# The fp32 products of 32 single rows: two weight tiles in one burst of 16 instead of one tile in a burst of 8

## The chip, the cores and the metric

One Trainium2 chip, one of its cores. The kernel is one launch. The time is device microseconds of one execution; the median of three executions of the kernel before is 1000.25 us (1000.03 to 1001.18). The profiled execution is another one, with its own time.

## What is computed

One inference step of a hybrid decoder layer for two groups of rows with the same weights: a prompt of 512 rows and a sample group of 8 x 4 = 32 rows. Cut to the matrix products that matter here:

```python
z = rms_norm(x, g_mix_pre) @ w_in            # q, k, v, o and gates of the mLSTM; dq, dk, dv of the attention
mix = concat(mlstm(z), diff_attention(z))    # with state and paged cache for the sample rows
x = x + rms_norm(mix @ w_out, g_mix_post)
x = x + rms_norm(mem_attend(rms_norm(x, g_mem_pre), mk, mv, w_mq, w_mo), g_mem_post)
u = rms_norm(x, g_ffn_pre) @ w_up            # (1024, 2*2752)
y = (silu(g) * a) @ w_down                   # after a causal depthwise convolution; (2752, 1024)
x = x + rms_norm(y, g_ffn_post)
```

Everything is fp32 in the reference. The outputs are the rows of both groups, the new caches and the states.

## The kernel before

**Two precisions.** For the 512 prompt rows a product is made of three fp32r matmuls. Each operand is split into a high part (a cast on ScalarE, line 142) and a low part (source minus high part, on VectorE or GpSimd, line 143); the three matmuls are high x high, high x low and low x high (lines 386 to 388 in `gemmA`, 1638 to 1640 in the down products). The 32 single rows, the sample group, do without the split: their products are plain fp32, from the weight tile as it came from memory.

**Weight tiles.** A weight tile is 256 x 512 (or 1024 x 128 for `gemmB`), 512 KB. The SP queue loads it into one of six stage buffers (`wst`, lines 227 and 246), ScalarE and VectorE split it into one of four slots (`wslot`). The class `Weights` holds a plan of all tiles in order: `W.get()` gives the next one, `W.free()` lets the plan run one tile further. A tile that `slotA` makes is the pair (slot, stage buffer), since the sample rows read the stage buffer. So a stage buffer is free once the split has read it and the sample products, if any, too.

**`gemmA`** makes a row-major projection of 512 columns: four weight tiles of two k each, for each tile the row blocks 0 to 3 of the prompt (128 rows each, 24 matmuls of 128 x 512 for a tile) and block 4, the sample rows. It is called for v (line 717), for dk, dq and dv (line 776), for the out projection and for mo (lines 1130 and 1136). Where a call is block-major (out, and the second half of mo) it follows another branch. `late=True` is used for the first half of mo.

**`sample_mm`** (line 366) makes the sample products of one weight tile: four fp32 products, two k times two column halves, of 128 x 256 each. Each goes to its own 32 partitions of one PSUM bank, so it uses 32 columns of TensorE's array. `sample_sum` (line 371) adds the four groups at the end.

**The ConvFFN** makes the up projection with `gemmB` (line 452; 440 for its first tiles) and after each group of four column tiles of the hidden width the down products of that group: two column halves (`n0`) of two weight tiles each, into five PSUM banks, one for each row block. There are six groups: four of them have four tiles and go through the loop `if not last`, so does the short one (tiles 20 and 21, third in order); the last one goes through `chunk`, block by block.

**What sets the order.** The program's order is a proposal only: the tile framework simulates a timeline and gives each engine its list of instructions, so work of several stages is interleaved on TensorE. In the stretch that makes dk, dq and dv it mixes their matmuls with the transposes of the rotated rows (line 742) and with the mLSTM head's chunks: mld (788, 789), mls (796), mlk (823), mlu (839), mli (857), mln (864), with mlD's activations on ScalarE (793) between.

The edit lengthens the file: three lines more in `gemmA`, nine by the end of the down products. A row of the changed kernel that reads L1647 is L1638 of before, L455 is 452, L745 is 742, L796 is 793, L842 is 839, L863 is 860.

## Time and profile before

| | us |
|---|---|
| median of three executions | 1000.25 |
| lowest, highest | 1000.03, 1001.18 |
| profiled execution, its time | 1001.39 |
| profiled execution, span from its first to its last instruction | 999.6 |
| mean granted TensorE clock | 0.988 of full speed |
| memory read and written | 112.22 MB, 16.93 MB |

The profile is one execution with every instruction's start. PE is TensorE's matmul pipe, PEld its weight loads, DVE VectorE, ACT ScalarE, POOL GpSimd, SP the queue that issues DMAs. A row of a timeline reads: start in us, us, engine, line and operation, output <- inputs, stationary operand, moving operand, count; in brackets the idle time before it and what ended it. The ends of matmuls are modelled, their starts are measured. A group of rows (by line and operation) gives count, busy time, the mean of one in ns and idle time ahead.

### The profile page before, as it was taken

What the parts mean: (1) busy time and instruction counts of PE and PEld (TensorE: products, weight loads), DVE (VectorE), ACT (ScalarE), POOL (GpSimd) and SP (SyncE); (2) the same over time, 40 slices, a digit from 0 to 9 for tenths busy, and PEclk for the clock granted to TensorE, in tenths of its full rate; (3) what the DMA queues carried; (4) which work ended last, traced back from release to release, by engine and by line L of the source; (5) the groups of instructions that cost most, each with busy time, mean ns of one, the idle gap of its engine ahead of it and who ended that gap; (6) DMA issues with size and microseconds to landing.
All of it is one profiled execution on the core that took longest, in us unless ns stands there. A gap on an engine that the chain in (4) does not pass through costs nothing.

```text
span 999.6 us, 17060 instructions
## 1 busy us (share of the span) xinstructions
PE 970.7 (97%) x6615; PEld 811.2 (81%) x6615; DVE 599.6 (60%) x1129; ACT 389.3 (39%) x746; POOL 196.1 (20%) x389
## 2 busy tenths in 40 slices
PE   8999999999799999999999999999999999999994
PEld 5899777889555778998767789989987997997983
DVE  5835324643586457643653578827848685775677
ACT  5654313434376447633552444242212222222232
POOL 6610000112332114500000264301101110010115
PEclk9999999999799999999999999999999999999997
DMA  8950234151634167785851673143143214215013
GB/s 278 296 162 14 72 85 130 43 183 55 176 109 136 61 210 233 250 260 166 277 214 43 195 237 107 43 129 91 41 115 87 84 46 127 90 42 145 25 47 110
DMA packets 120401, 130.26 MB, mean 130 GB/s; under 512 B 8423, under 2 KB 85832, under 8 KB 120320
## 3 DMA queue, kind: packets, MB, share of 16 engines
q1 hardware_dynamic: 114136, 125.69, 41.0%
q10 hardware_dynamic: 6184, 3.48, 1.2%
q8 instruction: 52, 0.85, 0.4%
q14 instruction: 29, 0.24, 0.1%
HBM read 112.22 MB, written 16.93 MB: 129 GB/s over the span
## 4 chain that ended last, share of the span: by engine, by line
PE 84%; DMA 5%; DVE 5%; issue 2%; POOL 1%; ACT 1%; SPq 0%; DVEq 0%; POOLq 0%; ACTq 0%
PE mm L452 31%; PE mm L386 6%; PE mm L387 6%; PE mm L388 6%; PE mm L440 5%; PE mm L1638 4%; PE mm L1640 4%; PE mm L1639 4%; PE mm L366 3%; PE sda L1179 2%; PE tpk L1384 2%; PE cpo L1365 1%; PE sca L1335 1%; PE ssc L1394 1%; PE oda L1205 1%
## 5 line engine op out<-in xcount | busy, mean ns | idle before, releaser
L142 ACT CAST wslot<-wst 128x1024 fp32r<-128x1024 f32 (+1 forms) x127 | 131.1, 1036 | 280.2 <-issue 81.5
L452 PE MATMUL mm<-fT,wslot 128*128 128x256 f32 (+1 forms) x1872 | 235.7, 288 | 0.0
L452 PEld LDWEIGHTS mm<-fT,wslot 128*128 128x128 f32 x1872 | 234.7, 188 | 0.7 <-issue 0.4
L143 DVE TENSOR_TENSOR wslot<-wst,wslot 128x1024 fp32r<-128x1024 f32 (+1 forms) x127 | 155.0, 1223 | 107.0 <-ACT wslot L142 106.9
L1638 PE MATMUL mm<-wslot,act 128*128 128x512 f32 (+1 forms) x176 | 70.7, 409 | 0.0
L1639 PE MATMUL mm<-wslot,act 128*128 128x512 f32 (+1 forms) x176 | 69.5, 395 | 0.0
L1640 PE MATMUL mm<-wslot,act 128*128 128x512 f32 (+1 forms) x176 | 69.0, 397 | 0.0
L1545 POOL COPY cvo<-u 128x2 f32<-128x2 f32 x43 | 16.2, 377 | 222.9 <-DVE u L1543 222.9
L386 PE MATMUL mm<-wslot,hT 128*128 128x512 f32 x128 | 51.9, 408 | 0.0
L452 PE MATMUL mm<-hT,wslot 128*128 128x288 f32 (+1 forms) x384 | 51.4, 290 | 0.0
L387 PE MATMUL mm<-wslot,hT 128*128 128x512 f32 x128 | 51.2, 400 | 0.0
L388 PE MATMUL mm<-wslot,hT 128*128 128x512 f32 x128 | 50.7, 397 | 0.0
L452 PEld LDWEIGHTS mm<-hT,wslot 128*128 128x128 f32 x384 | 48.9, 188 | 0.9 <-issue 0.8
L1638 PEld LDWEIGHTS mm<-wslot,act 128*128 128x128 f32 (+1 forms) x176 | 33.1, 189 | 17.7 <-issue 8.6
L1540 DVE TENSOR_TENSOR u<-mm,rsb 128x256 f32<-128x256 f32 x43 | 18.1, 423 | 43.5 <-PE mm L452 43.4
L1640 PEld LDWEIGHTS mm<-wslot,act 128*128 128x128 f32 (+1 forms) x176 | 33.0, 188 | 7.5
L1639 PEld LDWEIGHTS mm<-wslot,act 128*128 128x128 f32 (+1 forms) x176 | 33.1, 188 | 6.5
L1557 ACT ACTIVATE c<-c 128x560 f32<-128x560 f32 x21 | 14.1, 672 | 56.8 <-DVE c L1551 56.7
L1551 DVE SCALAR_TENSOR_TENSOR c<-u,cvT,c 128x560 f32<-128x560 f32 x43 | 34.3, 798 | 0.8
L1550 DVE SCALAR_TENSOR_TENSOR c<-u,cvT,c 128x560 f32<-128x560 f32 x43 | 34.1, 793 | 0.1
L1651 DVE TENSOR_TENSOR yp<-mm,yp 128x512 f32<-128x512 f32 x40 | 27.3, 688 | 9.5 <-PE mm L1640 9.4
L386 PEld LDWEIGHTS mm<-wslot,hT 128*128 128x128 f32 x128 | 24.0, 188 | 10.3 <-issue 5.8
(458 smaller groups left out, 1879.5 us busy)
## 6 DMA issues: line engine op xcount, KB each, us to landing
wst<-in_w_up_dram SPq DMA_DIRECT2D x42, 512.0 KB
wst<-in_w_in_dram SPq DMA_DIRECT2D x28, 512.0 KB
wst<-in_w_down_dram SPq DMA_DIRECT2D x20, 512.0 KB
wst<-in_cache_mem_k_dram SPq DMA_DIRECT2D x16, 512.0 KB
vt<-in_cache_mem_v_dram SPq DMA_DIRECT2D x8, 1024.0 KB
wst<-in_w_mk_dram SPq DMA_DIRECT2D x8, 512.0 KB
xb<-in_x_prompt_dram SPq DMA_DIRECT2D x8, 512.0 KB
wst<-in_cache_dk_dram SPq DMA_DIRECT2D x16, 256.0 KB
```

The costliest lines, as they stand in the source:

```text
L142: nc.scalar.copy(out=hi, in_=src)
L143: (eng or nc.vector).tensor_tensor(out=lo, in0=src, in1=f32(hi), op=SUB)
L386: mm(ps[b], lhsT=xt.hi(k, c0, c0 + n), rhs=s[:, 0, kk, :], start=(k == 0), stop=False)
L387: mm(ps[b], lhsT=xt.hi(k, c0, c0 + n), rhs=s[:, 1, kk, :], start=False, stop=False)
L388: mm(ps[b], lhsT=xt.lo(k, c0, c0 + n), rhs=s[:, 0, kk, :], start=False, stop=(k == nk - 1))
L440: mm(ps, lhsT=s[:, l, k, :], rhs=x(k, c0, c1), start=(k == 0 and j == 0), stop=(k == 7 and j == 2))
L452: mm(ps[i], lhsT=s[:, l, k, :], rhs=x(k, c0, c1), start=(k == 0 and j == 0), stop=(k == 7 and j == 2))
L1550: STT(out=c, in0=u[:, 1:EXT - 1], scalar=w[1], in1=c, op0=MUL, op1=ADD)
L1551: STT(out=c, in0=u[:, 0:EXT - 2], scalar=w[0], in1=c, op0=MUL, op1=ADD)
L1638: mm(ps, lhsT=t[:, 0, c0:c0 + P], rhs=s[:n, 0, i % 2, :], start=st, stop=False)
L1639: mm(ps, lhsT=t[:, 0, c0:c0 + P], rhs=s[:n, 1, i % 2, :], start=False, stop=False)
L1640: mm(ps, lhsT=t[:, 1, c0:c0 + P], rhs=s[:n, 0, i % 2, :], start=False, stop=en)
```

## The change

In `gemmA` outside the block-major branch the sample products of a weight tile are not issued when the tile comes, but kept in `behind`, and issued for two tiles when the second has come (k = 2 and k = 6). In the late form they are issued at k = 5 for all but the last tile kept, and at the end for the others. In the down products `one` keeps block 4's tiles in the same way and issues them at the second tile; the loops call it for block 4 only where i is even, once a weight tile. The number of products, their operands, and the bank and partitions that they go to are unchanged.

```diff
@@ gemmA
                     if 4 in blocks:
                         behind.append((k, s))
-                        if not late:
-                            one(4, *behind.pop(0))
+                        if k % 4 == 2 and not late:
+                            while behind:
+                                one(4, *behind.pop(0))
                 for b in blocks:
                     if b < 4:
                         one(b, k, s)
                 if k % 2 == 1:
-                    if len(behind) > 1:
-                        one(4, *behind.pop(0))
+                    if k == 5:
+                        while len(behind) > 1:
+                            one(4, *behind.pop(0))
                     if not late or k > 1:
                         W.free()
                 yield sum(0.64 if b < 4 else 0.43 for b in blocks)
             for k, s in behind:
                 one(4, k, s)
+            if behind:
                 W.free()
@@ down products
+        behind = []
+
         def one(b, ps, i, s):
...
             if b == 4:
-                if i % 2 == 0:
-                    sample_mm(ps, [acs[i], acs[i + 1]], s[1], st, i == nk - 2)
+
+                behind.append((i, s))
+                if i % 4 == 2 or i == nk - 2:
+                    for j, t in behind:
+                        sample_mm(ps, [acs[j], acs[j + 1]], t[1], j == 0, j == nk - 2)
+                    behind.clear()
                 return
...
                     for b in sorted(allb, reverse=i % 2 == 0):
-                        one(b, ps[b], i, s)
+                        if b < 4 or i % 2 == 0:
+                            one(b, ps[b], i, s)
...
-            for i in range(nk):
+            for i in range(0, nk, 2 if b == 4 else 1):
                 one(b, ps, i, wd[(n0 and nk // 2) + i // 2])
```

How the instructions stand on the engines, at three places. A name such as wst_6809 is one buffer of a tile, x4 a run of four equal rows; one row of L366 is one fp32 product.

TensorE at the start of the first down group, before: mm_7062 is the sample bank of the first column half, wst_6809 its first weight tile.

```order
L452 MATMUL mm_6984<-fT01_6087,wslot_6735 128x288
L366 MATMUL mm_7062<-wst_6809,acs_6607 32x256 x2
L366 MATMUL mm_7062<-wst_6809,acs_6615 32x256 x2
L1638 MATMUL mm_7061<-wslot_6810,act_6279 128x512
L1639 MATMUL mm_7061<-wslot_6810,act_6279 128x512
L1640 MATMUL mm_7061<-wslot_6810,act_6279 128x512
```

And after the change, where wst_6876 is the second weight tile of the same half:

```order
L1649 MATMUL mm_7058<-wslot_6810,act_6279 128x512
L366 MATMUL mm_7062<-wst_6809,acs_6607 32x256 x2
L366 MATMUL mm_7062<-wst_6809,acs_6615 32x256 x2
L366 MATMUL mm_7062<-wst_6876,acs_6757 32x256 x2
L366 MATMUL mm_7062<-wst_6876,acs_6899 32x256 x2
L1649 MATMUL mm_7060<-wslot_6877,act_6280 128x512
L1647 MATMUL mm_7059<-wslot_6877,act_6280 128x512
L1648 MATMUL mm_7059<-wslot_6877,act_6280 128x512
```

The first tile's products have moved from the group's first place to the second tile's, behind 29 fp32r matmuls.

TensorE at the end of dq, where the first sample products of dv (bank mm_1877) stand. Before:

```order
L386 MATMUL mm_1600<-wslot_1492,hT01_255 128x512
L387 MATMUL mm_1600<-wslot_1492,hT01_255 128x512
L388 MATMUL mm_1600<-wslot_1492,hT11_256 128x512
L366 MATMUL mm_1877<-wst_1630,xts_195 32x256 x4
L366 MATMUL mm_1877<-wst_1673,xts_195 32x256 x4
L864 MATMUL mln_1765<-vN_576,mlD_1428 128x129 x2
L742 MATMUL tpz_1808<-cpk_87,zq_1800 128x128 x4
```

After; wst_1626 and wst_1673 are dv's first two tiles:

```order
L386 MATMUL mm_1874<-wslot_1674,hT00_244 128x512
L387 MATMUL mm_1874<-wslot_1674,hT00_244 128x512
L366 MATMUL mm_1877<-wst_1626,xts_195 32x256 x4
L366 MATMUL mm_1877<-wst_1673,xts_195 32x256
L745 MATMUL tpz_1867<-cpk_87,zq_1856 128x32 x4
L842 MATMUL mlu_1892<-vN_576,wk_1699 128x129 x2
L366 MATMUL mm_1877<-wst_1673,xts_195 32x256 x3
L388 MATMUL mm_1874<-wslot_1674,hT10_245 128x512
```

The eight products stood together ahead of dv's fp32r matmuls; they now stand among them, and transposes and an mlu stand inside the run.

ScalarE in the dq stage, before: the casts (L142) are of dv's first three weight tiles, L793 is mlD of an mLSTM chunk.

```order
L744 COPY dkT<-tpz 128x4x128
L142 CAST wslot<-wst 128x1024
L744 COPY dkT<-tpz 128x4x32
L142 CAST wslot<-wst 128x1024
L793 ACTIVATE mlD<-mld,gt_1119 128x128 x4
L142 CAST wslot<-wst 128x1024
L464 COPY zq<-mm 128x512
```

And after:

```order
L747 COPY dkT<-tpz 128x4x128
L142 CAST wslot<-wst 128x1024
L747 COPY dkT<-tpz 128x4x32
L142 CAST wslot<-wst 128x1024 x2
L796 ACTIVATE mlD<-mld,gt_1119 128x128 x4
L863 ACTIVATE num<-mli,gt_1119 128x129 x2
L467 COPY zq<-mm 128x512
```

The third cast stands ahead of mlD's activations, where it stood behind them. On the SP queue the loads of dv's third and fourth tile stand behind all five stores of dk's rows, where the stores and loads alternated. GpSimd's order is the same.

## The prediction

> **What bounds the kernel now.** I read the page's busy times first, then its chain of waits. The first row is busy time and share of the span by engine; the other two are the chain that ended last, by engine and by line.

> ```profile
> PE 970.7 (97%) x6615; PEld 811.2 (81%) x6615; DVE 599.6 (60%) x1129; ACT 389.3 (39%) x746; POOL 196.1 (20%) x389
> ```
> ```profile
> PE 84%; DMA 5%; DVE 5%; issue 2%; POOL 1%; ACT 1%; SPq 0%; DVEq 0%; POOLq 0%; ACTq 0%
> PE mm L452 31%; PE mm L386 6%; PE mm L387 6%; PE mm L388 6%; PE mm L440 5%; PE mm L1638 4%; PE mm L1640 4%; PE mm L1639 4%; PE mm L366 3%; PE sda L1179 2%; PE tpk L1384 2%; PE cpo L1365 1%; PE sca L1335 1%; PE ssc L1394 1%; PE oda L1205 1%
> ```

> TensorE is busy for 97% of the span and 84% of the chain is its own work. But a share over the span says nothing of the stages that the change touches, so I asked for the busy time in windows. Columns: the window in us, its length, PE, PEld, DVE, ACT and POOL busy with their counts, the granted clock, the DMA share, GB/s.

> ```profile
> 97.00:225.00 128.00, 128.00 (x733) 98.23 (x726) 55.43 (x136) 40.38 (x76) 11.46 (x17) 1.00 0.36 102
> 253.00:285.00 32.00, 25.48 (x172) 16.00 (x172) 21.57 (x68) 15.42 (x48) 12.88 (x17) 0.79 0.55 165
> 259.00:273.00 14.00, 10.38 (x64) 6.46 (x65) 7.68 (x28) 1.88 (x6) 4.00 (x6) 0.51 0.68 204
> 640.00:960.00 320.00, 320.00 (x2212) 287.10 (x2211) 211.44 (x359) 81.71 (x99) 31.30 (x154) 1.00 0.29 81
> ```

> The projections v, dk, dq and dv lie in 97 to 225, the four down groups that change in 640 to 960. In both TensorE is never idle. So a nanosecond that its stream loses there is a nanosecond of the end, as long as nothing else becomes late. How many products there are does not change; the question is what a *burst* of them costs, and this the timeline shows.

> **What a burst costs.** Columns: start us, us, engine, line, operation. The profile records each fp32 product as two matmuls, so "x8" is four products, the four column groups of one weight tile. I call such a set of up to four a set.

> ```profile
> 649.06 0.39 PE L1639 MATMUL mm<-wslot,act 128*128 128x512 f32 x1
> 649.29 0.40 PE L1640 MATMUL mm<-wslot,act 128*128 128x512 f32 x1
> 649.62 0.64 PE L366 MATMUL mm<-wst,acs 128*32 128x256 f32 x8
> 650.18 0.50 PE L1638 MATMUL mm<-wslot,act 128*128 128x512 f32 x1
> 650.52 0.40 PE L1639 MATMUL mm<-wslot,act 128*128 128x512 f32 x1
> ...
> 658.40 0.40 PE L1640 MATMUL mm<-wslot,act 128*128 128x512 f32 x1
> 658.74 1.07 PE L366 MATMUL mm<-wst,acs 128*32 128x256 f32 x16
> 659.74 0.50 PE L1638 MATMUL mm<-wslot,act 128*128 128x512 f32 x1
> 660.07 0.39 PE L1639 MATMUL mm<-wslot,act 128*128 128x512 f32 x1
> ```
> ```profile
> 550.59 0.40 PE L388 MATMUL mm<-wslot,oT 128*128 128x512 f32 x1
> 550.91 2.80 PE L366 MATMUL mm<-wst,xts 128*32 128x256 f32 x48
> 553.64 0.50 PE L386 MATMUL mm<-wslot,oT 128*128 128x512 f32 x1
> 553.98 0.39 PE L387 MATMUL mm<-wslot,oT 128*128 128x512 f32 x1
> ```

> Ends are modelled, so I count from start to start. Two fp32r matmuls follow each other by 0.23 us (649.06 to 649.29). Around the burst of one set, 649.29 to 650.52 is 1.23; two steps of 0.23 belong to the fp32r matmuls, and 0.77 is the price of the burst. The burst of two sets: 658.40 to 660.07 is 1.67, less 0.46 is 1.21. That of six sets ("x48"): 550.59 to 553.98 is 3.39, less 0.46 is 2.93. From one set to six, (2.93 - 0.77) / 5 = 0.43 us for each further set, and two sets (1.21) lie on that line. What is left, 0.77 - 0.43 = 0.34 us, is paid once a burst: the last fp32r matmul before it, the first set and the two matmuls behind it start 0.33 apart where 0.23 is usual. So the kernel before already holds the merged form, and a merge saves 0.34 us.

> Two more readings decide how broken sets count. Columns as above.

> ```profile
> 162.56 0.62 PE L366 MATMUL mm<-wst,xts 128*32 128x256 f32 x2
> 163.11 0.50 PE L386 MATMUL mm<-wslot,hT 128*128 128x512 f32 x1
> ```
> ```profile
> 182.48 0.61 PE L857 MATMUL mli<-Cst,qT 128*128 128x129 f32 x4
> 182.93 0.61 PE L864 MATMUL mln<-vN,mlD 128*128 128x129 f32 x4
> ```
> ```profile
> 209.75 0.61 PE L857 MATMUL mli<-Cst,qT 128*128 128x129 f32 x4
> 210.28 0.62 PE L366 MATMUL mm<-wst,xts 128*32 128x256 f32 x4
> 210.84 0.60 PE L864 MATMUL mln<-vN,mlD 128*128 128x129 f32 x3
> ```

> One product alone holds the stream for 0.55 us (162.56 to 163.11), four for 0.56 (649.62 to 650.18): a set costs the same full or not, so breaking a set in two costs 0.43 more. And between fp32 matmuls of the mLSTM head the fixed part is smaller: 209.75 to 210.84 is 1.09, less 0.45 for the L857 group itself (182.48 to 182.93) is 0.64, less 0.43 for the set leaves 0.21.

> **The change part by part**, by the bursts in the order of the two kernels, each a number of products:

> - v: 4,4,4,4 becomes 8,8. Two bursts fewer, the same four sets: -0.68.
> - dk: the same, -0.68.
> - dq: 6,2,3,1,4 becomes 4,4,7,1. The scheduler drops other work between them, so the joint bursts do not stay whole. One burst fewer; six sets (2+1+1+1+1) become five: -0.34 - 0.43 = -0.77.
> - dv: 8,4,2,2 becomes 5,3,1,2,5. Here the order is worse than before: one burst and two sets more (5 to 7): +0.34 + 0.86 = +1.20.
> - the first half of mo: 2,2,4,24 becomes 8,24. Two bursts and one set fewer: -0.68 - 0.43 = -1.11.
> - the down products: each of the four large groups goes from 4,4,8 to 8,8, one burst fewer each: -1.36. The 8 before is the second column half, whose two tiles the scheduler already runs in one burst, so only half of what the diff seems to promise is there to be had. The group of two tiles and the last group keep their bursts, as does the out projection.

> Together ten bursts fewer (41 to 31) and no set fewer (-1 + 2 - 1): -3.4 us. If every one of the ten were worth only the 0.21 of the mLSTM rows, it would be -2.1. These are the two ends; I take 0.34, because dq and dv come to no burst in sum, and those of v, dk, mo and the downs lie between 512-wide fp32r matmuls like the row it is from.

> What else moves. The fp32 stage tile of the first of two weight tiles is read later, in the downs by one tile's fp32r work, 24 x 0.23 = 5.5 us and a little more. So it comes free later, and the load that takes its buffer starts later. The distance between load and use hides that nearly everywhere: the down tiles are loaded while 200 and more L452 matmuls run, and wait in the stage. The place that I trust least is dv's third tile. Its load before on the SP queue, its cast and what stands beside it on ScalarE:

> ```profile
> 153.73 0.37 SPq L227 DMA_DIRECT2D wst<-in_w_in_dram  x1
> ```
> ```profile
> 177.26 1.14 ACT L793 ACTIVATE mlD<-mld,gt 128x128 f32<-128x128 f32 x4 [1.10 <-PE mld L789]
> 179.69 1.05 ACT L142 CAST wslot<-wst 128x1024 fp32r<-128x1024 f32 x1 [1.29 <-PE mm L388]
> ```

> Issued at 153.73, cast at 179.69: 26 us, and the cast waited for its slot (L388), not for the load. In the changed kernel the load waits for the first joint dq burst and stands on the SP queue behind all five stores of dk rather than three; and on ScalarE its cast stands ahead of the four mlD activations (L793), not behind them. From that burst to the fp32r matmul that frees the slot the new order has 12 fp32r matmuls, one more set, a group of transposes and two of mlu: about 4.6 us. What a load takes, at its quickest and slowest in the chain of waits:

> ```profile
> 20.84 9.51 DMA wst<-in_w_in_dram
> 585.34 5.03 DMA wst<-in_w_up_dram
> ```

> So it lands between 0.4 and 5 us after the slot is free, and the cast, the mlD activations behind it and VectorE's steps come that much later. TensorE needs mlD for mln (L864, 182.93 above):

> ```profile
> 176.54 0.40 PE L788 MATMUL mld<-mlE,ones_r 128*128 128x512 f32 x1
> ```
> ```profile
> 178.44 0.69 DVE L797 TENSOR_TENSOR mlD<-mls,mlD 128x512 f32<-128x512 f32 x1 [1.01 <-ACT mlD L793]
> 180.78 1.23 DVE L143 TENSOR_TENSOR wslot<-wst,wslot 128x1024 fp32r<-128x1024 f32 x1 [1.05 <-ACT wslot L142]
> ```

> Before, 182.93 - 176.54 = 6.4 us lie between mld and mln; the changed order has two fp32r matmuls fewer there (-0.46), a burst of two sets (0.64 + 0.43) and one of a single product (0.64): 7.6. The chain needs 1.05 for the cast, 1.23 for VectorE's low part (the activations, 1.14, run beside it) and 0.69 for its mlD step: 3.0. So the load may be 4.6 us late before TensorE waits. With the quick load 4 us are to spare, with the slowest it is short by half a microsecond. I cost it at nothing and keep up to 2 us for the range.

> ScalarE and VectorE get no other work, and GpSimd keeps its order. Nothing of the DMA traffic changes but its times.

> **Sum.** The profiled execution took 1001.39 us, its span 999.6; with 3.4 less that is 998.0, the span 996.2. The median of the runs shown is 1000.25 (1000.03 to 1001.18), 1.14 under the profiled one, so the forecast is 1000.25 - 3.4 = 996.9 us; by the lower end 998.2.

> **Rivals.**

> *A wait in the reordered dq and dv stage eats the gain* (chance 0.20): the late tile above. For it: TensorE has no idle in 97 to 225 today, and a new order of five engines in a chain of small steps (mld, mlD, mln, the rotations of dq) has many places that are close; dv already loses 1.20 by its order. Against it: the wait that I followed has 4 us left with a quick load. Its point is a load of over 9 us, or SP held by the dk stores as long; its price, by a step of the size of the cast or two, is 1 to 3 us, 998.0 to 999.9, and I name 999.

> *The stretch at half clock* (slower: chance 0.10). The windows above show it: in 259 to 273 the granted clock is 0.51. Ahead of it TensorE waits for the Cs loads, and in one other place, at the start of the ConvFFN, it waits in small pieces at full clock:

> ```profile
> 258.53 0.41 PE L949 MATMUL mlsi<-Cs,qzm 128*32 128x128 f32 x2 [1.60 <-DMA Cs<-in_state_ml_C_dram]
> 260.81 1.92 PE L949 MATMUL mlsi<-Cs,qzm 128*32 128x128 f32 x26 [1.88 <-DMA Cs<-in_state_ml_C_dram]
> ...
> 580.15 0.49 PE L1513 MATMUL rsb<-cpk,rsd 128*128 128x128 f32 x2 [1.07 <-DVE ht L319]
> 581.75 0.39 PE L440 MATMUL mm<-fT,wslot 128*128 128x256 f32 x1 [0.33 <-ACT wslot L142]
> ```

> The mechanism: at 579 to 582 the change lets mo end earlier and its stage tile come free later, the first w_up cast comes late, and the idle there grows from 1.4 us (1.07 + 0.33) and some tenths towards the 3.5 us (1.60 + 1.88) that stand before the slow stretch. From there on a second stretch of 14 us would run at 0.51 in dense fp32r work: 14 x 0.49 = 6.9 us, 1003.8. Against it: the first of these waits is for VectorE's ht and not for a tile, and mo's frees come in the same number. The other way round, the waits for Cs could fall so that the stretch at 259 is cut short: its 10.38 busy us at half clock are worth 5 us at most, and 996.9 would become some 994; 0.03. [...]

> *The merge saves nothing* (chance 0.05): a second set would wait with its weight loads until the first has run, the 0.34 would move inside the burst, and two sets cost 2 x 0.77 = 1.54. The sets come to no change in sum, so the time would stay at 1000.25. Against it: the burst at 658.74 measures 1.21 instead of 1.54, and that at 550.91 2.93 instead of 4.6; only bursts in a new place could behave otherwise. [...]

> **How the numbers follow.** My forecast, ten bursts at 0.21 to 0.34, has 0.62; its own range is 996.2 to 998.3. The wait has 0.20, the second slow stretch 0.10, no saving 0.05, a shorter slow stretch 0.03. Less than 0.2% (2.0 us) cannot be told from no change here; faster means below 998.25. The forecast gives nearly all of its 0.62 to faster, the wait 0.04, the short stretch 0.03: 0.68. Same: the wait's other 0.14, no saving 0.05 and a rest of the forecast 0.02: 0.21. Slower: 0.10, and 0.01 for a wait far longer than I see. The range 995.2 to 1000.3 takes in the forecast, the wait and no saving, and leaves out the two cases of the clock.

> **What would show it.** Right: eight bursts "x16" of L366 in the down windows, each about 1.0 us from its start to the next fp32r matmul, and none of "x8" but in the group of two tiles; v and dk with two bursts each; PE busy in 97 to 225 and 640 to 960 without a gap; the start of the first down group about 2 us earlier, and the last group's about 3.4. The down groups' row of L366 keeps its count and its mean:

> ```profile
> L366 PE MATMUL mm<-wst,acs 128*32 128x256 f32 x168 | 13.8, 388 | 0.0
> ```

> Wrong: idle before L857, L864 or L742 in the dq and dv stage (the wait); a granted clock under 1 anywhere but near 257 to 271 (the second rival); a burst of two sets that holds the stream for 1.5 us (the third); the start of the ml states at 225 not 0.9 us earlier, which is what v, dk, dq and dv come to (-0.68 - 0.68 - 0.77 + 1.20).

## The result and the profile after

The change makes the kernel faster: 998.24 us median against 1002.04 of the kernel before, measured beside it (22 runs each), ratio 0.9963, 95% interval 0.9952 to 0.9974, so 2.6 to 4.8 us, 3.7 in the middle. The forecast was 3.4 us (0.9967). The profiled execution's span is 994.8 us, 4.8 shorter than the 999.6 of before.

The busy row of the changed kernel:

```profile
PE 967.3 (97%) x6615; PEld 812.5 (82%) x6615; DVE 600.0 (60%) x1129; ACT 389.0 (39%) x746; POOL 194.1 (20%) x389
```

TensorE works 3.4 us less (970.7 to 967.3) with the same 6615 matmuls. The windows of the stages, columns as before:

```profile
97.00:225.00 128.00, 128.00 (x747) 100.75 (x746) 55.66 (x136) 41.58 (x79) 9.53 (x18) 1.00 0.33 102
640.00:960.00 320.00, 320.00 (x2222) 287.17 (x2223) 211.92 (x361) 81.01 (x98) 29.59 (x154) 1.00 0.29 81
```

Both are still without a gap, and hold more matmuls than before: 747 against 733, 2222 against 2212. That is what a denser stream looks like. A merged burst in the first down group:

```profile
649.18 0.40 PE L1649 MATMUL mm<-wslot,act 128*128 128x512 f32 x1
649.51 1.07 PE L366 MATMUL mm<-wst,acs 128*32 128x256 f32 x16
650.51 0.50 PE L1649 MATMUL mm<-wslot,act 128*128 128x512 f32 x1
650.85 0.39 PE L1647 MATMUL mm<-wslot,act 128*128 128x512 f32 x1
```

649.18 to 650.85 is 1.67 us, to a hundredth what the merged burst of the kernel before took at 658.40.

**Where the time went, stage by stage.** The span alone misleads here, as the table shows. For each TensorE matmul (the n-th of its line) I took its start in one trace less its start in the first trace of before, and the median over a quiet stretch between two stages. The difference of two neighbours is what the stage between them gained (negative) or lost. The rows are all profiled executions: the kernel before twice more, the change three times, and the other experiments.

| us against the first trace of before | start, to 95 | v, dk, dq, dv | ml states and attention, to 530 | mo | ConvFFN's start | four large down groups | short group | sum |
|---|---|---|---|---|---|---|---|---|
| before, e9 | -1.21 | 0.00 | -1.17 | 0.00 | +0.43 | 0.00 | 0.00 | -1.95 |
| before, e10 | -0.18 | 0.00 | +0.28 | 0.00 | -0.04 | -0.01 | 0.00 | +0.05 |
| the change | -1.13 | -1.07 | -0.29 | -0.35 | -0.42 | -1.50 | 0.00 | -4.76 |
| the change, e6 | -0.58 | +0.40 | -0.70 | -0.63 | +0.23 | -1.50 | 0.00 | -2.78 |
| the change, e11 | -0.48 | -1.07 | +0.26 | -0.75 | +0.58 | -1.50 | 0.00 | -2.96 |
| e1, downs only | -0.37 | 0.00 | -0.05 | 0.00 | -0.12 | -1.50 | 0.00 | -2.04 |
| e2, projections only | -1.35 | +0.41 | -0.91 | -0.54 | -0.21 | 0.00 | 0.00 | -2.60 |
| e3, dv tile by tile | -1.90 | -1.68 | -2.56 | -0.82 | +1.36 | -1.50 | 0.00 | -7.10 |
| e4, downs in 16 | -0.89 | +0.41 | -0.85 | -0.68 | +0.36 | -2.82 | -0.56 | -5.03 |
| e5, mo's bank | -0.75 | -1.07 | +0.05 | -0.75 | +0.30 | -1.50 | 0.00 | -3.73 |
| e7, e3 and e4 | -0.11 | -1.67 | -1.91 | -0.63 | -0.09 | -2.82 | -0.56 | -7.79 |
| e8, more merged | -1.23 | -2.30 | -0.64 | -0.82 | +1.47 | -2.82 | -0.56 | -6.90 |

The change works in the projections, in mo and in the down groups. The other three stages (the start, the ml states with the attention, the ConvFFN's start) scatter from one execution to the next, and they do so in the kernel before too: over its three executions by 1.21, 1.45 and 0.47 us. Of the 4.8 us between the two first spans 1.8 lie in these three.

### The profile page after: what moved, and what is told of

Read it like the earlier page. It is cut to its first block, busy times and chain, and to the rows that moved or that the text cites. A ratio compares the mean times of both kernels' runs of the same rounds, so it can differ in the third digit from the quotient of the medians.

```text
span 994.8 us, 17056 instructions
## 1 busy us (share of the span) xinstructions
PE 967.3 (97%) x6615; PEld 812.5 (82%) x6615; DVE 600.0 (60%) x1129; ACT 389.0 (39%) x746; POOL 194.1 (20%) x389
## 4 chain that ended last, share of the span: by engine, by line
PE 85%; DVE 6%; DMA 5%; issue 2%; ACT 1%; POOL 1%; SPq 0%; DVEq 0%; POOLq 0%; ACTq 0%
PE mm L455 31%; PE mm L386 6%; PE mm L387 6%; PE mm L388 6%; PE mm L443 5%; PE mm L1647 4%; PE mm L1649 4%; PE mm L1648 4%; PE mm L366 3%; PE sda L1182 2%; DMA xb<-x_d 2%; PE tpk L1387 2%; PE cpo L1368 1%; PE sca L1338 1%; PE ssc L1397 1%
## 5 line engine op out<-in xcount | busy, mean ns | idle before, releaser
L142 ACT CAST wslot<-wst 128x1024 fp32r<-128x1024 f32 (+1 forms) x127 | 131.1, 1036 | 274.5 <-issue 74.4
L143 DVE TENSOR_TENSOR wslot<-wst,wslot 128x1024 fp32r<-128x1024 f32 (+1 forms) x127 | 155.1, 1223 | 92.3 <-ACT wslot L142 91.7
L386 PE MATMUL mm<-wslot,hT 128*128 128x512 f32 x128 | 51.8, 408 | 0.0
L455 PE MATMUL mm<-hT,wslot 128*128 128x256 f32 (+1 forms) x384 | 51.4, 290 | 0.0
L387 PE MATMUL mm<-wslot,hT 128*128 128x512 f32 x128 | 50.8, 397 | 0.0
L388 PE MATMUL mm<-wslot,hT 128*128 128x512 f32 x128 | 50.6, 398 | 0.0
L386 PEld LDWEIGHTS mm<-wslot,hT 128*128 128x128 f32 x128 | 24.1, 188 | 6.6 <-issue 2.1
```

What stands on the lines that cost most here:

```text
L142: nc.scalar.copy(out=hi, in_=src)
L143: (eng or nc.vector).tensor_tensor(out=lo, in0=src, in1=f32(hi), op=SUB)
L386: mm(ps[b], lhsT=xt.hi(k, c0, c0 + n), rhs=s[:, 0, kk, :], start=(k == 0), stop=False)
L387: mm(ps[b], lhsT=xt.hi(k, c0, c0 + n), rhs=s[:, 1, kk, :], start=False, stop=False)
L388: mm(ps[b], lhsT=xt.lo(k, c0, c0 + n), rhs=s[:, 0, kk, :], start=False, stop=(k == nk - 1))
L455: mm(ps[i], lhsT=s[:, l, k, :], rhs=x(k, c0, c1), start=(k == 0 and j == 0), stop=(k == 7 and j == 2))
```

## The experiments

**e1: the down products alone.** `gemmA` as before.

```diff
-                        if k % 4 == 2 and not late:
-                            while behind:
-                                one(4, *behind.pop(0))
+                        if not late:
+                            one(4, *behind.pop(0))
...
```

> The projections as before, only the down products merged. Burst theory (a removed burst is worth 0.34 us, a further set 0.43): v, dk, dq, dv and mo stand as before, so 97 to 585 us shows no shift but what the waits for DMAs at the start and for Cs do; each of the four large down groups is 0.34 to 0.38 us shorter, 1.4 to 1.5 in all, time 0.9985 to 0.9986 of before. Rival (the gain comes from waits outside the changed stages, as the start's -1.13 us and the ml states' -0.73 us in the trace of the change suggest): those two places shift here too or not at all, whatever the bursts do, and the down groups alone decide nothing of the median. The mo burst of 48 records stays at 2.42 us inside (no wait for a bank).

Measured: the four groups -0.38, -0.37, -0.37 and -0.37, nothing in the projections and in mo, mo's burst 2.42 us inside. Ratio 0.9992 (0.9975 to 1.0008): the interval reaches both the forecast 0.9985 and 1, so the median tells nothing here; the stages do. Each removed burst is worth 0.37 us in the downs, and to a hundredth the same in every run that has the change.

**e2: the projections alone.** The down products as before.

> Only the projections merged, the down products as before. Burst theory: v and dk -0.7 each, dq and dv together +0.4 to +0.5, mo -0.3 (its -0.7 less a wait of 0.4 for a PSUM bank inside the burst of 24 products); in sum -1.2 to -1.4 us, and no shift at all from 645 to 960 us. Rival (waits elsewhere): the sum over the projections is about 0 and the median moves by what start and ml states do.

Measured: nothing from 645 to 960 us, as expected; mo -0.54. But v, dk, dq and dv together *lost* 0.41 us with the same order of instructions there that gained 1.07 in the trace of the change. Ratio 0.9976 (0.9967 to 0.9985). The bursts were not the cause: they have the same lengths to 0.01 us. The granted clock was 0.5 for 3.41 us from 96.05 us, which neither first trace shows. That led to e6, and to the section at the end.

**e3: dv tile by tile.** The change otherwise.

```diff
-                        if k % 4 == 2 and not late:
+                        if not late and (k % 4 == 2 or not pair):
...
-    F.add(gemmA(hT, 8, allb, ev_dk), gemmA(hT, 8, allb, ev_dq), gemmA(hT, 8, allb, ev_dv),
+    F.add(gemmA(hT, 8, allb, ev_dk), gemmA(hT, 8, allb, ev_dq), gemmA(hT, 8, allb, ev_dv, pair=False),
...
```

> The change, but dv's sample products issued tile by tile as before. The order built has dv in bursts of 10, 2, 1, 3 (four bursts, six sets) instead of 5, 3, 1, 2, 5 (five bursts, seven sets), all else in the same bursts. Burst theory: one burst and one set fewer, 0.34 + 0.43 = 0.77 us (0.6 if the burst among fp32 matmuls counts 0.21) less than the change in 97 to 225 us, 0.9955 to 0.996 of before. If instead a set is paid by its number of products, nothing changes there (16 products both times).

Measured: -1.68 where the change has -1.07, so 0.61 less for one burst and one set, the lower of the two forecasts (0.43 + 0.21 = 0.64); ratio 0.9943 (0.993 to 0.9955). In these stages it is better to leave dv unmerged in the program, because the scheduler then merges ten of its products by itself. The first burst of dv in e3's timeline:

```profile
181.74 0.61 PE L867 MATMUL mln<-vN,mlD 128*128 128x129 f32 x4
182.28 1.49 PE L366 MATMUL mm<-wst,xts 128*32 128x256 f32 x20
183.70 0.66 PE L745 MATMUL tpz<-cpk,zq 128*128 128x128 f32 x4
```

And in the change, where transposes and mlu stand inside the eight:

```profile
194.25 0.40 PE L387 MATMUL mm<-wslot,hT 128*128 128x512 f32 x1
194.57 1.05 PE L366 MATMUL mm<-wst,xts 128*32 128x256 f32 x10
195.56 0.43 PE L745 MATMUL tpz<-cpk,zq 32*128 32x32 f32 x4
195.92 0.71 PE L842 MATMUL mlu<-vN,wk 128*128 128x129 f32 x4
196.56 0.63 PE L366 MATMUL mm<-wst,xts 128*32 128x256 f32 x6
197.12 0.50 PE L388 MATMUL mm<-wslot,hT 128*128 128x512 f32 x1
```

The run of 20 records (ten products, three sets) holds the stream from 182.28 to 183.70, 1.42 us; those of ten and six records (eight products, also three sets, since the second tile's four are broken in one and three) 0.99 and 0.56, 1.55 us, and pay the entry twice. The ratio of e3 holds more than this 0.61. With dv made tile by tile, in e3, e7 and e8, the scheduler also gave TensorE another order in the attention: of its 361 matmuls from 272 to 320 us 59 stand at another place in the order. In all the other traces the order from 226 to 530 us is that of the kernel before, and in these three too but for that stretch. Between 279 and 300 us these three gain 1.32, 1.32 and 1.33 us, and no other trace moves there by more than 0.01: TensorE's wait of 1.05 us for kT and one of 0.38 us for pda (L1183 of before), which all others have, are gone. So some 1.3 us of e3's gain come from this new order, a side effect of the edit, and not from the bursts.

**e4: one burst for both column halves of a down group**, into one bank, each half in its own 256 columns.

```diff
-                behind.append((i, s))
-                if i % 4 == 2 or i == nk - 2:
-                    for j, t in behind:
-                        sample_mm(ps, [acs[j], acs[j + 1]], t[1], j == 0, j == nk - 2)
+                behind.append((i, s, ps))
+                if last and (i % 4 == 2 or i == nk - 2) or len(behind) == nk:
+                    for j, t, p in behind:
+                        sample_mm(p, [acs[j], acs[j + 1]], t[1], j == 0, j == nk - 2)
                     behind.clear()
...
+                if n0 == 0:
+                    bank = mmp()
+                ps[4] = sam[n0] = bank[:, n0 // 2:n0 // 2 + 256]
...
```

The additions of the sample rows (`add_y(4, ...)`) move behind both halves.

> The change, and in the down products one burst for both column halves of a group: 16 products (four sets) into one bank, so 8,8 becomes 16 in the four large groups and 4,4 becomes 8 in the short one. Burst theory: four times another 0.34 = 1.36 us, and in the short group 0.3 to 0.6 more, so 1.7 to 1.9 us under the change, 0.9945 of before. Rival (stage buffers): four of six stage buffers are then held through the group, the next w_up loads start up to 13 us later, and TensorE waits at the start of the next up projection; then the groups show idle and the time is that of the change or above it.

Measured: -0.71, -0.69, -0.72 and -0.71 in the large groups, 0.33 each beyond the change's, and -0.56 in the short one; no wait in the up projections behind. The rival with the stage buffers falls. Ratio 0.9943 (0.9931 to 0.9956).

**e5: another bank for mo's second half.** In the trace of the change mo gained 0.35 us, not the 1.11 forecast. Its burst of 24 products shows where a part of that went:

```profile
547.34 0.40 PE L388 MATMUL mm<-wslot,oT 128*128 128x512 f32 x1
547.67 1.07 PE L366 MATMUL mm<-wst,xts 128*32 128x256 f32 x16
548.93 1.93 PE L366 MATMUL mm<-wst,xts 128*32 128x256 f32 x32 [0.19 <-DVE y L1092]
550.79 0.50 PE L386 MATMUL mm<-wslot,oT 128*128 128x512 f32 x1
551.13 0.39 PE L387 MATMUL mm<-wslot,oT 128*128 128x512 f32 x1
```

547.34 to 551.13 is 3.79 us where the same burst took 3.39 before: there is a wait behind its first eight products, for VectorE's y (L1092). VectorE, in the same stretch:

```profile
547.05 1.23 DVE L143 TENSOR_TENSOR wslot<-wst,wslot 128x1024 fp32r<-128x1024 f32 x1 [7.90 <-ACT wslot L142]
548.19 1.88 DVE L1092 TENSOR_TENSOR y<-mm,gb 128x512 f32<-128x512 f32 x3
```

The first y reads a bank of mo's first half behind a weight tile's low part. The eight products are the first half's, the sixteen the second half's, and these need a free bank. The merged bursts bring TensorE to the second half earlier, in this trace before that bank is read out: VectorE begins the first y at 548.19, behind the burst's start at 547.67, where in the kernel before it began at 549.65, ahead of the burst at 550.91. e5 gives them a bank of the other pool:

```diff
-                ps[b] = mmp()
+                ps[b] = at("mm") if bank4 and b == 4 else mmp()
...
```

> The change, with the sample bank of mo's second half taken from the other PSUM pool, so that nothing of the first half has to be read out before it. Bank theory: the burst of 24 products in mo runs without a gap, 2.42 us from its first to its last start as in the kernel before, where the change's own run had 2.82 and the run with the projections alone 2.63; mo from 530 to 565 us is 0.75 us shorter than before. Rival (the gap is a weight load or the stage tile that comes late): the gap of 0.2 to 0.4 us stays.

Measured, one execution: no gap, and mo -0.75.

```profile
548.05 0.40 PE L388 MATMUL mm<-wslot,oT 128*128 128x512 f32 x1
548.38 2.80 PE L366 MATMUL mm<-wst,xts 128*32 128x256 f32 x48
551.11 0.50 PE L386 MATMUL mm<-wslot,oT 128*128 128x512 f32 x1
551.44 0.39 PE L387 MATMUL mm<-wslot,oT 128*128 128x512 f32 x1
```

This alone shows less than it seems: the change itself had no gap in e11 (-0.75 there too), nor had e3. The gap is there in some executions (0.40, 0.21, 0.18, 0.12, 0.07 us) and absent in others, so a bank that comes free just in time is the reading that fits the first trace's releaser, and e5 agrees with it; the one run without a gap does not prove it.

**e6 and e11: the changed kernel again; e9 and e10: the kernel before again.**

> The changed kernel itself once more. Phase theory (the half clock comes in units of 3.41 us on a grid whose phase differs from one execution to the next, and a unit is granted at half where the stretch of small matmuls at 93 to 95.5 us fills the one before it): either no slow unit at 96 us and 97 to 225 us is 1.07 us shorter than before, or one and it is 0.4 longer; the stages where the clock is full repeat within 0.05 us (each down group -0.37 to -0.38). Rival (the waits for Cs and the start are part of what the change does): the start's -1.13 us and the ml states' -0.73 us repeat.

> The kernel before once more, for the clock. Grid theory (the clock is halved for units of 3.41 us on a grid that is fixed in one execution and lies elsewhere in the next; a unit is slow where the one before it held 2.5 us or more of small matmuls or waits): the kernel before has the same two stretches, at 94 to 97 and at 578.7 to 582.4 us, and gets a slow unit behind one of them whenever the grid lies so; in this run the overlap with the grid must agree with what is granted. Rival (only the change brings slow units outside 250 to 275 us): none, whatever the grid.

> As the last one: a third execution of the kernel before with its own grid. Grid theory: a slow unit behind 94 to 97 or 578.7 to 582.4 us if and only if one unit of the grid held 2.5 us or more of that stretch. Rival: none, whatever the grid.

> A third execution of the changed kernel. Grid theory: the four large down groups again -0.37 to -0.38 each, 97 to 225 us again -1.07 if no slow unit falls at 96 us or +0.4 if one does, mo -0.75 plus a gap of 0 to 0.4 in its burst of 24; the rest of the difference to the kernel before is made by the start, by the waits for Cs and by slow units. Rival: the start and the ml states repeat their -1.13 and -0.73 us.

Measured: the rows of the table show it. The stages of the change repeat to 0.01 us wherever the clock is full, but for mo's gap; start, ml states and ConvFFN's start do not repeat, in neither kernel (the start of before: 0, -1.21, -0.18). Three executions of the change give -4.76, -2.78 and -2.96 against the same trace of before, and another execution of before -1.95. The 0.73 us is what the ml states alone seemed to gain in the first trace of the change, up to 279 us; e6 has 1.16 there and e11 0.60, and the kernel before 0.99 in e9 and 0.08 in e10. So neither this nor the start's 1.13 is shown to be the change's. A part of the 0.73 may still be: all nine traces with merged projections gain 0.36 or more there, and of the other three (e1, e9, e10) only e9 does. e6 has the slow unit at 96 us and loses 0.40 in the projections, e11 has none and gains 1.07, as the grid theory said; its "if and only if" failed at the edge, which the last section takes up.

**e7: e3 and e4 together.** Both edits as shown.

> The two steps that gave more than the change put together: dv tile by tile and one burst of 16 in each down group. Burst theory: 0.6 to 0.77 us less than the change in 97 to 225 us, 0.34 less in each large down group and 0.56 less in the short one, 2.5 to 2.7 in all; 0.9935 of before. Rival (the stage buffers held long make the up projection wait at another place): less than the sum.

Measured: -1.67, and -2.82 and -0.56: the steps add up, nothing is lost between them. Ratio 0.9935 (0.9914 to 0.9955).

**e8: also one burst of 16 for each of v and dk**, with e5's bank.

```diff
-                        if not late and (k % 4 == 2 or not pair):
+                        if not late and (k == 6 or (pair < 2 and k % 4 == 2) or not pair):
...
-    run(gemmA(hT, 8, allb, ev_v))
+    run(gemmA(hT, 8, allb, ev_v, pair=2))
...
```

dk's call gets `pair=2` in the same way, dv's `pair=0`, which is what `pair=False` was in e3.

> As the last one, with all four weight tiles of v and of dk in one burst of 16 (two bursts fewer) and mo's other bank. Burst theory: another 0.68 us in 97 to 160 us and 0 to 0.4 in mo: 0.993 of before. Rival (in the projections all four stage tiles are held until the last one's products, and the tiles behind come late): idle on TensorE in dk or dq, and the gain there is gone.

Measured: -2.30 in the projections, 0.63 beyond e7, for two bursts fewer; no idle in dk or dq; mo without a gap. A burst of 16 products (four sets):

```profile
112.40 0.40 PE L388 MATMUL mm<-wslot,hT 128*128 128x512 f32 x1
112.73 1.93 PE L366 MATMUL mm<-wst,xts 128*32 128x256 f32 x32
114.59 0.50 PE L386 MATMUL mm<-wslot,hT 128*128 128x512 f32 x1
114.93 0.40 PE L387 MATMUL mm<-wslot,hT 128*128 128x512 f32 x1
```

112.40 to 114.93 is 2.53, less 0.46 is 2.07; the line of the prediction gives 0.77 + 3 x 0.43 = 2.06. Ratio 0.9924 (0.9904 to 0.9943), 994.63 us median: the fastest here by its median, though the interval overlaps that of e7, 0.9961 of the changed kernel if the two ratios are divided (0.9924 / 0.9963), with 23 bursts instead of 31.

## Why the prediction was right

The forecast ratio was 0.9967, the measured 0.9963. By its steps:

- *What bounds the kernel*: right. TensorE had no idle in the two stages, before or after, and what a burst lost was lost at the end.
- *A burst costs 0.34 once and 0.43 for each set*: right. Merged bursts take 1.67 us around themselves as read from before, four sets 2.07. The removed burst measured 0.37 to 0.38 in the downs' large groups (0.34 forecast; the burst taken away there stood behind the 288-wide L452, not between fp32r matmuls), 0.33 more in e4, 0.31 each in e8.
- *Sets count full or not, and a burst among the mLSTM's fp32 matmuls costs 0.21*: borne out by e3, which removed one of each and gained 0.61 in the projections. As the next two points show, this price does not hold beside every fp32 product.
- *v and dk*: -0.68 each. Over v the shift grew by 0.45 us and over dk by 0.69, in e11 and e5 as well. dk is as forecast. Of v's two merges the second gave 0.37 and the first only 0.09 (the shift is -1.13 ahead of v, -1.21 behind the first merged burst, -1.58 behind the second). The burst that the first merge took away stood behind the 4-row products of dps. Its place before, then in the change; and the same for dk's first burst:

```profile
96.40 0.36 PE L698 MATMUL dps<-Bc,tb 4*128 4x8 f32 x2
96.69 0.64 PE L366 MATMUL mm<-wst,xts 128*32 128x256 f32 x8
```
```profile
95.27 0.36 PE L701 MATMUL dps<-Bc,tb 4*128 4x8 f32 x2
95.56 0.50 PE L386 MATMUL mm<-wslot,hT 128*128 128x512 f32 x1
```
```profile
123.61 0.60 PE L823 MATMUL mlk<-cpk,kT 128*128 128x128 f32 x4
124.14 0.64 PE L366 MATMUL mm<-wst,xts 128*32 128x256 f32 x8
```
```profile
122.03 0.60 PE L826 MATMUL mlk<-cpk,kT 128*128 128x128 f32 x4
122.38 0.48 PE L386 MATMUL mm<-wslot,hT 128*128 128x512 f32 x1
```

From dps to what follows it is 0.29 us with the burst and 0.29 without, so the step into the burst cost nothing there, and the fp32r matmul that now follows dps pays a step out of its own (95.56 to the next at 95.91, 0.35 where 0.23 is usual). From mlk it is 0.53 with the burst and 0.35 without, and taking that burst away gave 0.37, although it too stood behind fp32 products. So 0.34 for v's first burst was too much, and the prediction did not look where it stood.

- *dq and dv*: +0.43 in sum, +0.07 measured, in all of these three traces. The count of bursts and sets was right, but three of the nine bursts of before stood between fp32r matmuls and none of the nine of after does, since the scheduler put them beside the transposes and the mLSTM's products. Three times (0.34 less 0.21) is 0.39, which would be the difference. But this sum rests on the one row of the smaller price and on e3, and dk's first burst speaks against so simple a rule. So the term was mis-sized by 0.36, and the cause is argued, not shown.
- *mo*: -1.11 forecast, -0.75 measured without a gap. This term was mis-sized twice. Between its first two half sets stood the short transpose L1479 (L1482 now), which the sum took for nothing. The kernel before, then the change, where it is moved out and pays for a place of its own:

```profile
540.53 0.63 PE L366 MATMUL mm<-wst,xts 128*32 128x256 f32 x4
541.09 0.23 PE L1479 MATMUL cvp<-cpk,cr 20*128 20x20 f32 x1
541.25 0.63 PE L366 MATMUL mm<-wst,xts 128*32 128x256 f32 x4
```
```profile
538.37 0.40 PE L386 MATMUL mm<-wslot,oT 128*128 128x512 f32 x1
538.70 0.23 PE L1482 MATMUL cvp<-cpk,cr 20*128 20x20 f32 x1
538.86 0.50 PE L387 MATMUL mm<-wslot,oT 128*128 128x512 f32 x1
539.19 0.39 PE L388 MATMUL mm<-wslot,oT 128*128 128x512 f32 x1
```

538.37 to 539.19 is 0.82, less 0.46 is 0.36, and that is the difference. And a wait of 0 to 0.40 us for a bank came on top, of which the prediction had nothing.

- *The downs*: -1.36 forecast, -1.50 measured in every run.
- *The late tile of dv costs nothing*: right. Its load was issued at 167.57, and its cast, the second row, waited for the slot (L388) and not for the load:

```profile
170.92 1.05 ACT L142 CAST wslot<-wst 128x1024 fp32r<-128x1024 f32 x1 [2.71 <-PE mm L388]
172.31 1.05 ACT L142 CAST wslot<-wst 128x1024 fp32r<-128x1024 f32 x1 [0.35 <-PE mm L388]
173.27 1.13 ACT L796 ACTIVATE mlD<-mld,gt 128x128 f32<-128x128 f32 x4
```
```profile
174.94 0.69 DVE L800 TENSOR_TENSOR mlD<-mls,mlD 128x512 f32<-128x512 f32 x1 [0.31 <-PE mls L799]
```
```profile
180.00 0.61 PE L867 MATMUL mln<-vN,mlD 128*128 128x129 f32 x4
```

mlD was done at 175.63, mln began at 180.00: 4.4 us to spare, where the prediction had 4. The first rival did not come.

- *The merge saves nothing*: fallen, by every burst above: two sets cost 1.21 us and four 2.07, so a further set costs 0.43 us, not 0.77.
- *A second slow stretch at the ConvFFN's start*: its place was right and its story wrong. It comes in the kernel before as well (e9), in units of 3.41 us and not of 14, and one unit costs half a microsecond to one there (+0.43 against -0.04 in the kernel before, +0.23 to +0.58 against -0.42 in the change), not 6.9. The prediction named a granted clock under 1 away from 257 to 271 us as a sign against it. That sign came in e6 and e11, and cost far less than it allowed for.

The terms measured are -1.07 - 0.75 - 1.50 = -3.3 us, less the gap and the slow units where they come; the median says 2.6 to 4.8. That the sum of 3.4 fits so well is partly luck: v's 0.23 and mo's 0.36 were too much, dq and dv's 0.36 and the downs' 0.14 too little. Two of its signs show the same: in the first trace the first down group starts 3.3 us earlier and the last 4.8, not 2 and 3.4, because the stages that scatter lie in between.

## What to carry to other kernels

Where an engine is busy throughout, look for the price of a switch between two kinds of work in rows that are already there: this kernel held merged and unmerged bursts, and their difference gave the whole forecast. Read the order that is built, not the program: here the scheduler had merged some bursts by itself and broke others that the program joined, and in dv it did better without the edit. An edit can also change the order in a stage that it does not touch, as dv's did with 1.3 us of the attention. And compare profiles stage by stage, with two or three executions of the same kernel beside them, since differences of 2 us lay in stages that the change does not touch.

## What the runs showed of the hardware

**And it fell where TensorE was not idle.** Windows cut at the grid of e6, then at that of e11, the changed kernel both times:

```profile
93.02:96.43 3.41, 3.41 (x28) 3.15 (x28) 1.71 (x4) 1.62 (x3) 0.00 (x0) 1.00 0.00 0
96.43:99.84 3.41, 3.41 (x16) 2.33 (x15) 0.16 (x1) 0.00 (x0) 0.00 (x0) 0.50 0.00 0
```
```profile
92.80:96.21 3.41, 3.41 (x30) 3.18 (x29) 1.39 (x3) 1.62 (x3) 0.00 (x0) 1.00 0.00 0
96.21:99.62 3.41, 3.41 (x22) 2.58 (x22) 0.48 (x3) 0.00 (x0) 0.00 (x0) 1.00 0.00 0
```

In e6 the unit from 93.02 counts as busy throughout; 2.52 us of it are five small fp32 products (gtp) and the 4-row products of dps. The next unit is granted half the clock, and the projections lose 1.47 us (+0.40 against -1.07). The unit ahead of the 13.65 us at half clock had idle time: TensorE was busy for 1.44 of its 3.41 us in the first trace of before (255.71 to 259.12), for 2.15 in the first of the change (252.36 to 255.77). In e6, and in e2 and e4 in the same place, a unit with matmuls of 4 rows and without idle time was followed by half the clock too. At the ConvFFN's start the kernel before, in e9, has the same with a unit that is half idle:

```profile
576.89:580.30 3.41, 1.69 (x7) 1.10 (x8) 3.41 (x4) 2.70 (x5) 2.68 (x5) 1.00 0.51 144
580.30:583.71 3.41, 3.41 (x17) 3.41 (x17) 3.41 (x7) 1.66 (x3) 1.40 (x4) 0.50 0.99 273
```

Over 13 traces every slow stretch behind these two places began right behind a unit that held 2.5 us or more of the small matmuls and waits, and none began behind a unit that held 2.49 us or less. In e3 and e8 the stretch at the ConvFFN's start went on for a second unit, though the first held only 0.5 us of them. But not every unit with 2.5 us was followed by a slow one: in e11 the unit from 92.80 held the same 2.52 us and the clock stayed full, and so it did in e9 near 96 us and, with 2.54, at the ConvFFN's start in the first trace of the change. So a bound is seen from one side only, and what decides near 2.5 us stays open. Near 96 us three of the nine traces with merged projections have a slow unit and none of the other four; at the ConvFFN's start it is seven of the nine against one of the four. Whether the change shifts these odds would take many more executions than these.
